# Moving work from VectorE to GpSimd and ScalarE in a two-layer diffusion trunk on one core

## The chip, the cores and the metric

The kernel runs on one core of one Trainium2 chip. A core has five engines with instruction queues of their own: TensorE (PE, matrix products; PEld is its weight load), VectorE (DVE), ScalarE (ACT), GpSimd (POOL) and SyncE (SP), which here issues every DMA. The metric is the device time of one execution in microseconds, lower is better. A time is the median of several runs; the profile comes from one further execution.

## The reference

Two layers work on 1024 latent tokens and 256 context tokens of width 1024, in float32. Cut to what matters:

```python
sh1, sc1, g1, sh2, sc2, g2 = modulation(c, w_ada[i], b_ada[i])       # silu(c) @ w_ada + b_ada, in six parts
h = modulate(rms_norm(x, norm1_g[i]), sh1, sc1)                      # the context likewise, with c_ctx
a_z, bq, bk, bv, cq, ck, cv = split_proj(h @ w_in[i])
out_a = chunk_gmlp(a_z, a_ws[i], a_bs[i])                            # gating in chunks of 128
out_b = window_attn_latent(q_b, k_b, v_b, k_bc, v_bc, b_sink[i])     # 8 heads, window 128, sink
o_c = diff_attn_latent(q_c, k_c, v_c, k_cc, v_cc, lam)               # 4 heads, two softmax maps each
x = x + g1 * (concat([out_a, out_b, out_c]) @ w_out[i])
x = x + g2 * conv_ffn(modulate(rms_norm(x, norm2_g[i]), sh2, sc2), w_up[i], conv_w[i], conv_b[i], w_down[i])
```

`conv_ffn` projects up to 2 x 2816 features, applies a depthwise convolution of width 3, multiplies silu(gate) by the value half and projects down. The context takes the same steps in layer 0 and gives keys and values only in layer 1.

## The kernel before

**Weights.** A float32 weight block comes by DMA into `raw` (three buffers). ScalarE rounds it into a high part, and a second engine subtracts the high part from the block to get the low part; both go into one tile `wsp` (three buffers, tag `ws`). `wunit` (L111) does this; its engine for the subtraction is VectorE everywhere, through the helper `sub` (L108). A product is the sum of three: high by high, high by low, low by high (`mm3`, L123), so TensorE needs a low part only at the third product of each block of 128 rows. Activations (`h`, `g`, keys, queries) are split alike.

**Modulation.** In layer 0 `mod_chunk` (L135) multiplies 2 MB chunks of `w_ada` on TensorE with a 32-column `cpad`, four 512 KB pieces a chunk, and four row blocks side by side in the array. In layer 1 `mod_wide` (L156) has VectorE multiply-add each 128 x 512 block with a column of `cpad` into an accumulator, eight blocks for each chunk and condition, then transpose and reduce it. It runs inside the MLPs of layer 0's groups b and c, called by `hook` at a given feature tile: four chunks with two conditions there, eight chunks with one here.

**Opening.** One 2 MB chunk of modulation, two context tiles (`load_x`, L322: load, square sum, transpose, store), three more chunks, the small setup, then `norms` for five tiles, `setup2` (rope tables and small constants by many small DMAs and table writes), then the input projection `ipset` with column blocks 3 and 2 of `w_in`.

**Norm.** `norm_tile` (L196) squares a tile on ScalarE, adds its eight blocks with one VectorE reduction (`red`, L203), transposes, takes a power of -0.5 on GpSimd, makes a diagonal matrix, spreads it by a product, multiplies, applies scale and shift, and splits into high and low.

**Attention.** `units_b` and `units_c` compute scores into PSUM; `negmax` (L471) copies them negated to SBUF with a running minimum on VectorE; ScalarE takes the exponential; TensorE transposes it and multiplies with the values. In `units_b` the reciprocal row sums become 128 x 128 diagonals (L569, on VectorE), used by a product (L606) after the outputs of the second half of the heads. In `units_c` the tail takes a power on GpSimd (L738).

**MLP.** `mlp` (L817) works on a group of columns (three groups in each layer, `G0` and `G1`, 256 to 516 columns wide). For each of 22 feature tiles `up` makes two products, evicts with the convolution's centre tap on ScalarE (L837) and the two side taps on VectorE (L841, L844), and forms `g`. `down` takes three or four feature tiles at a time: eight units of `w_down` of 384 or 512 columns a partition, each with 9 or 12 products and an addition into the residual `xg` (L869).

**Order.** The Tile framework places the instructions on each engine's queue with a simulated timeline, in the order of the program where several are ready; so the MLP of group a fills in beside the later tiles' attention, in both layers. Each queue then runs in that fixed order, and an instruction that waits holds what stands behind it.

## Time and profile before

| | |
|---|---|
| median of three runs | 3370.29 us (3367.59 to 3371.93) |
| profiled execution, time | 3366.29 us |
| profiled execution, span from first to last instruction | 3364.5 us |
| TensorE busy, mean granted clock | 3160.1 us (94%), 0.971 |
| VectorE busy | 2473.2 us (74%) |
| ScalarE busy | 1669.9 us (50%) |
| GpSimd busy | 368.0 us (11%) |
| DMA | 499.5 MB, 148 GB/s over the span |

A row of the groups reads: line, engine, operation, output<-inputs by the program's names with their shapes, count, then busy time in us and the mean of one in ns, then idle time of the engine just before them and what ended it. A row of the windows has the stretch, its length, the busy time of TensorE, its weight loads, VectorE, ScalarE and GpSimd with their instruction counts, the granted clock of TensorE (1.00 is full), the share of time that the DMA engines were busy, and what they moved. A row of a timeline has start, length, engine, line, operation, names and shapes, and in brackets the idle time before it with what ended it. A DMA issue is a row of the queue SPq. The profile's chain of waits covers only the later part of the span in this case, so stages are read by windows and waits.

### The profile page before, as it was taken

What the parts mean: (1) busy time and instruction counts of PE and PEld (TensorE: products, weight loads), DVE (VectorE), ACT (ScalarE), POOL (GpSimd) and SP (SyncE); (2) the same over time, 40 slices, a digit from 0 to 9 for tenths busy, and PEclk for the clock granted to TensorE, in tenths of its full rate; (3) what the DMA queues carried; (4) which work ended last, traced back from release to release, by engine and by line L of the source; (5) the groups of instructions that cost most, each with busy time, mean ns of one, the idle gap of its engine ahead of it and who ended that gap; (6) DMA issues with size and microseconds to landing.
All of it is one profiled execution on the core that took longest, in us unless ns stands there. A gap on an engine that the chain in (4) does not pass through costs nothing. (4 is left out here: it accounts for less than half of the span.)

```text
span 3364.5 us, 54283 instructions
## 1 busy us (share of the span) xinstructions
PE 3160.1 (94%) x19695; PEld 2760.8 (82%) x19695; DVE 2473.2 (74%) x5666; ACT 1669.9 (50%) x2931; POOL 368.0 (11%) x386
## 2 busy tenths in 40 slices
PE   6999988899998999999999899999999999999999
PEld 4777656787897898998999777767887789999998
DVE  4776765776888895879866578758887686676666
ACT  3555545655555443634334345557565564444443
POOL 0444200100000000100001144101000000000000
PEclk7999988899999999999999999999999999999999
DMA  9555795344442583377433555445555446334433
GB/s 270 172 157 156 222 272 149 100 117 131 126 125 78 169 250 111 103 206 210 131 93 110 161 146 159 126 142 142 155 149 148 114 124 194 112 113 135 132 115 111
DMA packets 766411, 499.50 MB, mean 148 GB/s; under 512 B 81480, under 2 KB 722368, under 8 KB 766144
## 3 DMA queue, kind: packets, MB, share of 16 engines
q1 hardware_dynamic: 766144, 496.03, 51.7%
q8 instruction: 156, 2.56, 0.3%
q14 instruction: 111, 0.91, 0.1%
HBM read 432.48 MB, written 63.44 MB: 147 GB/s over the span
## 5 line engine op out<-in xcount | busy, mean ns | idle before, releaser
L130 PE MATMUL z<-h,wsp 128*128 128x386 f32 (+3 forms) x5280 | 871.5, 318 | 12.5 <-DVE t L844 6.9
L130 PEld LDWEIGHTS z<-h,wsp 128*128 128x128 f32 x5280 | 819.4, 189 | 27.3 <-issue 9.6
L115 ACT ACTIVATE wsp<-raw 128x1024 fp32r<-128x1024 f32 (+2 forms) x660 | 555.8, 846 | 462.1 <-PE z L130 229.8
L109 DVE TENSOR_TENSOR wsp<-raw,wsp 128x1024 fp32r<-128x1024 f32 (+2 forms) x660 | 641.6, 974 | 86.6 <-ACT wsp L115 83.4
L130 PE MATMUL z<-g,wsp 128*128 128x386 f32 (+3 forms) x2640 | 459.9, 322 | 23.3 <-DVE xg L869 9.9
L130 PEld LDWEIGHTS z<-g,wsp 128*128 128x128 f32 x2640 | 416.5, 191 | 40.8 <-issue 13.2
L132 PE MATMUL z<-wsp,h 128*128 128x512 f32 x1584 | 408.3, 404 | 15.5 <-ACT wsp L115 7.3
L132 PEld LDWEIGHTS z<-wsp,h 128*128 128x128 f32 x1584 | 293.1, 192 | 84.7 <-ACT wsp L115 8.2
L130 PE MATMUL zS<-h,wsp 128*128 128x386 f32 (+1 forms) x2112 | 334.8, 314 | 8.0 <-DVE t L844 6.4
L130 PEld LDWEIGHTS zS<-h,wsp 128*128 128x128 f32 x2112 | 319.5, 191 | 10.6 <-issue 6.6
L837 ACT ACTIVATE t<-z,cw 128x386 f32<-128x386 f32 (+3 forms) x220 | 138.3, 629 | 247.2 <-PE z L130 243.8
L841 DVE SCALAR_TENSOR_TENSOR t<-z,cw,t 128x255 f32<-128x255 f32 (+3 forms) x264 | 132.7, 503 | 121.4 <-ACT t L837 120.8
L672 ACT ACTIVATE ec<-ec,nmc 128x1280 f32<-128x1280 f32 (+1 forms) x144 | 182.2, 1266 | 67.3 <-DVE ec L473 66.4
L130 PE MATMUL z<-oT,wsp 128*128 128x384 f32 (+2 forms) x1056 | 199.3, 336 | 3.1 <-DMA oT<-o_s 2.1
L473 DVE TENSOR_SCALAR_CACHE_REDUCE ec<-S,nmc 128x512 f32<-128x512 f32 (+1 forms) x256 | 156.8, 612 | 54.3 <-PE S L669 51.6
L130 PE MATMUL zS<-g,wsp 128*128 128x386 f32 (+1 forms) x1056 | 182.9, 317 | 12.0 <-DVE t L844 4.0
L130 PEld LDWEIGHTS z<-oT,wsp 128*128 128x128 f32 x1056 | 176.7, 189 | 12.0 <-DMA oT<-o_s 2.9
L669 PE MATMUL S<-Kc,qc 128*128 128x512 f32 (+1 forms) x400 | 158.7, 418 | 27.0 <-DVE ec L473 24.3
L869 DVE SCALAR_TENSOR_TENSOR xg<-z,mods,xg 128x384 f32<-128x384 f32 (+5 forms) x288 | 140.4, 501 | 58.0 <-PE z L130 57.8
L130 PEld LDWEIGHTS zS<-g,wsp 128*128 128x128 f32 x1056 | 162.7, 192 | 17.6 <-ACT wsp L115 4.6
L360 POOL TENSOR_TENSOR rs<-ss,cst 128x8 f32<-128x8 f32 (+1 forms) x76 | 116.2, 1529 | 366.6 <-DVE ss L358 293.3
L590 ACT ACTIVATE PT<-T 128x512 f32<-128x512 f32 (+1 forms) x168 | 94.7, 573 | 117.8 <-PE T L586 104.9
(245 smaller groups left out, 4450.5 us busy)
## 6 DMA issues: line engine op xcount, KB each, us to landing
raw<-in_w_up_dram SPq DMA_DIRECT2D x264, 512.0 KB
mraw<-in_w_ada_dram SPq DMA_DIRECT2D x96, 512.0 KB
raw<-in_w_down_dram SPq DMA_DIRECT2D x192, 256.0 KB
Kc<-qk_s SPq DMA_DIRECT2D x96, 320.0 KB
raw<-in_w_in_dram SPq DMA_DIRECT2D x52, 512.0 KB
raw<-in_w_out_dram SPq DMA_DIRECT2D x48, 512.0 KB
raw<-in_w_down_dram SPq DMA_DIRECT2D x104, 192.0 KB
qk_s<-st SPq DMA_DIRECT2D x18, 512.0 KB
```

The lines of the kernel that those rows point to most:

```text
L109: eng.tensor_tensor(out=lo, in0=src, in1=hi.bitcast(F32), op=ALU.subtract)
L115: act.activation(out=hl[:, 0], in_=raw, func=AF.Copy)
L130: pe.matmul(ps, w(i, k), h(j, k), start=s, stop=e)
L132: pe.matmul(ps, h(i, k), w(j, k), start=s, stop=e)
L360: pool.tensor_tensor(out=rs[:, :ns], in0=ss[:, 1, :ns], in1=mhalf[:, :ns], op=ALU.pow)
L473: dve.tensor_scalar(out=neg, in0=s_ap, scalar1=-1.0, scalar2=init, op0=ALU.mult, op1=ALU.min, accum_out=acc)
L590: act.activation(out=PT[:, :w_], in_=tp[:, :w_], func=AF.Copy)
L669: pe.matmul(S[:, :w_], q[:, m, ti * P:ti * P + P], K[m][:, o:o + w_], start=True, stop=True)
L672: act.activation(out=e[:, :nk], in_=e[:, :nk], func=AF.Exp, scale=-1.0, bias=acc, accum_out=l1[:, m, ti:ti + 1])
L837: act.activation(out=t[:, o:o + n], in_=ps[:, :n], func=AF.Identity, scale=cw[:, L, 1, ft:ft + 1], bias=cw[:, L, 3, ft:ft + 1])
L841: dve.scalar_tensor_tensor(out=t[:, o + b + 1:o + e], in0=ps[:, b:e - 1], scalar=cw[:, L, 0, ft:ft + 1], in1=t[:, o + b + 1:o + e], op0=AL ...
L869: dve.scalar_tensor_tensor(out=xs, in0=ps[:, b + o0:b + o1], scalar=mods[:, L, 40 + ct, s:s + 1], in1=xs, op0=ALU.mult, op1=ALU.add)
```

## The change

- A low part on GpSimd is made in pieces of 128 columns if it has more than 256 columns (before: more than 512). `mlp` and `prep` take the engine of the low part as an argument; three MLPs (layer 0 group a, layer 1 groups a and b) give GpSimd for `w_down`.
- The diagonals of L569 are made by GpSimd.
- In `mod_wide` the products are ScalarE's and the additions GpSimd's, through a tile with two buffers.
- In the norm the reduction over eight blocks is three additions of halves. The norm is split into a front and a back.
- In `mod_chunk` a piece is 256 rows by 512 columns instead of 512 by 256, two products of 512 columns for each piece.
- Opening: `setup` comes right after the first chunk; the fronts of the norms of tiles 8, 9 and 0 are done ahead; `w_in`'s column block 3 is asked for before the last of them, its fourth piece in a pool that now exists from the start; the convolution weights are loaded by `setup3`, after the first projections.

```diff
@@ wunit
-        if eng is pool and nk * ncol > 512:
+        if eng is pool and nk * ncol > 256:
@@ mod_chunk
-        for c in range(2):
-            for kth in range(2):
-                raw = mkraw()
-                c0 = ch * 512 + c * 256
-                sp.dma_start(out=raw, in_=a["w_ada"][L, kth * 512:kth * 512 + 512, c0:c0 + 256]
-                             .rearrange("(k p) c -> p k c", p=P))
-                for j in range(4):
-                    pe.matmul(ps[32 * j:32 * j + 32, c * 256:c * 256 + 256], cpad[:, 4 * kth + j, :], raw[:, j, :],
-                              start=(kth == 0), stop=(kth == 1))
+        for q in range(4):
+            raw = mkraw()
+            sp.dma_start(out=raw, in_=a["w_ada"][L, q * 256:q * 256 + 256, ch * 512:ch * 512 + 512]
+                         .rearrange("(k p) c -> p k c", p=P))
+            for i in range(2):
+                j = 2 * (q % 2) + i
+                pe.matmul(ps[32 * j:32 * j + 32, :], cpad[:, 2 * q + i, :], raw[:, i, :], start=(q < 2), stop=(q >= 2))
@@ mod_wide
-                        dve.tensor_scalar(out=acc[s], in0=raw[:, k], scalar1=c1, scalar2=None, op0=ALU.mult)
+                        act.activation(out=acc[s], in_=raw[:, k], func=AF.Identity, scale=c1)
                     else:
-                        dve.scalar_tensor_tensor(out=acc[s], in0=raw[:, k], scalar=c1, in1=acc[s],
-                                                        op0=ALU.mult, op1=ALU.add)
+                        pr = mktr()
+                        act.activation(out=pr, in_=raw[:, k], func=AF.Identity, scale=c1)
+                        pool.tensor_tensor(out=acc[s], in0=acc[s], in1=pr, op=ALU.add)
@@ norm_tile, now norm_front and norm_back
-            dve.tensor_reduce(out=red, in_=sq.rearrange("p k t -> p t k"), axis=AX.X, op=ALU.add)
+            for w_ in (4, 2):
+                dve.tensor_tensor(out=sq[:, 0:w_], in0=sq[:, 0:w_], in1=sq[:, w_:2 * w_], op=ALU.add)
+            dve.tensor_tensor(out=red, in0=sq[:, 0], in1=sq[:, 1], op=ALU.add)
@@ units_b, scores
-                            dve.tensor_scalar(out=dgs[ti][:, j], in0=ident, scalar1=ls[:, j:j + 1], scalar2=None,
-                                              op0=ALU.mult)
+                            pool.tensor_scalar(out=dgs[ti][:, j], in0=ident, scalar1=ls[:, j:j + 1], scalar2=None,
+                                               op0=ALU.mult)
@@ mlp, down (prep and w_out alike, with VectorE everywhere)
-                w = wunit(a["w_down"][L, fs[0] * P:fs[0] * P + nf * P, ct * P:ct * P + P], nf, P)
+                w = wunit(a["w_down"][L, fs[0] * P:fs[0] * P + nf * P, ct * P:ct * P + P], nf, P, eng=lo)
@@ norms
-        ahead = max(ahead, len(q))
+        ahead = 2 if pre else ahead
...
-            norm_tile(L, 0, xc, int(i >= NLT), h[:, 0], h[:, 1], mk, big, xc, ss, E_[eng[n % len(eng)]], add[n % len(add)])
+            if ss != "done":
+                norm_front(xc, mk, big, xc, ss)
+            norm_back(L, 0, xc, int(i >= NLT), h[:, 0], h[:, 1], E_[eng[n % len(eng)]], add[n % len(add)])
@@ opening
+    wx = mkpool("wx0", 1, "right")
...
     modset(0, (2,), ini, "mev", ini, "mraw", 16, mkz, mkU)
-    pre = [load_x(i, nwk, mkT) for i in (8, 9)]
+    setup(ini, mkU)
+
+    def load_norm(i):
+        xc, ss = load_x(i, nwk, mkT)
+        norm_front(xc, mkT, None, xc, ss)
+        return xc, "done"
+
+    pre = [load_norm(i) for i in (8, 9)]
     modset(0, (3, 0, 1), ini, "mev", ini, "mraw", 16, mkz, mkU)
-    setup(ini, mkU)
     mod_scale(0, 0)
+    w3 = inproj_w(0, 3, wx)
+    pre.append(load_norm(0))
...
     setup2(ini2, 0, mkU)
-    ipset(0, al, (3, 2))
+    ipset(0, al, (3, 2), w=w3)
+    setup3(ini2, 0, mkU)
@@ layer 0 group a, layer 1 groups a and b
-    mlp(0, G0[0], *x1, M, hook)
+    mlp(0, G0[0], *x1, M, hook, pool)
-    mlp(1, G1[0], *x1, M, hook)
+    mlp(1, G1[0], *x1, M, hook, pool)
-    mlp(1, G1[1], *st["x2"], M, hook)
+    mlp(1, G1[1], *st["x2"], M, hook, pool)
```

More of the change, by code (lines that the diff above doesn't have):

```diff
@@ L193, in mod_scale, with norm_front @@
                                      in1=g, op0=ALU.add, op1=ALU.mult)
-    def norm_tile(L, which, src, s, hi, lo, mkps, mkbig, f=None, ss=None, eng=pool, add='a'):
+    def norm_front(src, mkps, mkbig, f=None, ss=None):
         ms = sm.tile([P, 2], F32, tag="nms", name="nms")
@@ L216, in norm_tile, with norm_back @@
         dve.tensor_tensor(out=f, in0=src, in1=bc[:, 0:P].unsqueeze(1).to_broadcast([P, KT, P]), op=ALU.mult)
+        return f
+    def norm_back(L, which, f, s, hi, lo, eng=pool, add='a'):
         for k in range(KT):
@@ L224, in norm_tile @@
         sub(eng, lo, f, hi)
+    def norm_tile(L, which, src, s, hi, lo, mkps, mkbig, f=None, ss=None, eng=pool, add='a'):
+        norm_back(L, which, norm_front(src, mkps, mkbig, f, ss), s, hi, lo, eng, add)
     def setup_c(ini, ips):
@@ L309, in setup2, with setup3 @@
                                  op0=ALU.add, op1=ALU.subtract)
+    def setup3(ini, L, mkp):
         cr = ini.tile([2 * NFF, 4, P], F32, tag="cr", name="cr")
@@ L779, in prep_loads, with prep @@
         return xg, oT, [lambda k=k: load(k) for k in range(0, KT, 2)]
-    def prep(L, G, p, mp, pl=None):
+    def prep(L, G, p, mp, pl=None, lo=dve):
         wd = G["W"]
@@ L790, in prep @@
             for ct in range(KT):
-                w = wunit(a["w_out"][L][:, ct * P:ct * P + P], KT, P)
+                w = wunit(a["w_out"][L][:, ct * P:ct * P + P], KT, P, eng=lo)
                 ps = mkz()
@@ L815, in trunk, with mlp @@
     GB = 5
-    def mlp(L, G, xg, hT, halo, mp, hook=lambda f: None):
+    def mlp(L, G, xg, hT, halo, mp, hook=lambda f: None, lo=dve):
         halo()
@@ L968, in norms @@
         q = pre or [load(i) for i in tiles[:ahead]]
-        ahead = max(ahead, len(q))
+        ahead = 2 if pre else ahead
         for n, i in enumerate(tiles):
-            q += [load(j) for j in tiles[n + ahead:n + ahead + 1]]
+            q += [load(j) for j in tiles[len(q):n + ahead + 1]]
             xc, ss = q[n]
             h = hp.tile([P, 2, KT, P], F32R, tag="h", name="h")
-            norm_tile(L, 0, xc, int(i >= NLT), h[:, 0], h[:, 1], mk, big, xc, ss, E_[eng[n % len(eng)]], add[n % len(add)])
+            if ss != "done":
+                norm_front(xc, mk, big, xc, ss)
+            norm_back(L, 0, xc, int(i >= NLT), h[:, 0], h[:, 1], E_[eng[n % len(eng)]], add[n % len(add)])
             hts[i] = h
@@ L985, in modwide @@
                  lambda: p.tile([P, 512], F32, tag="mev", name="mev", bufs=2),
-                 lambda: p.tile([P, 512], F32, tag="mtr", name="mtr"))
+                 lambda: p.tile([P, 512], F32, tag="mtr", name="mtr", bufs=2))
     def modset(L, chs, evp, evt, rawp, rawt, rawb, mkps, mkpt):
@@ L990, in modset @@
             mod_chunk(L, ch, mkps, mkpt, evp.tile([P, 512], F32, tag=evt, name="mev", bufs=wb.get(evt, 1)),
-                      lambda: rawp.tile([P, 4, 256], F32, tag=rawt, name="mraw", bufs=rawb))
+                      lambda: rawp.tile([P, 2, 512], F32, tag=rawt, name="mraw", bufs=rawb))
     modset(0, (2,), ini, "mev", ini, "mraw", 16, mkz, mkU)
-    pre = [load_x(i, nwk, mkT) for i in (8, 9)]
+    setup(ini, mkU)
[4 more added lines that the diff above has]
+    pre = [load_norm(i) for i in (8, 9)]
     modset(0, (3, 0, 1), ini, "mev", ini, "mraw", 16, mkz, mkU)
-    setup(ini, mkU)
     mod_scale(0, 0)
+    w3 = inproj_w(0, 3, wx)
+    pre.append(load_norm(0))
     ini.release()
@@ L1000, in trunk @@
     wk = mkpool("wk0", 2, "right")
-    wx = mkpool("wx0", 1, "right")
     hts = {}
@@ L1034, in trunk @@
     mod_scale(0, 1)
-    wx.release()
     wk.release()
     hp.release()
+    wx.release()
     def attn(L, tiles):
@@ L1096, in hook @@
             setup2(ini, 1, mkT)
+            setup3(ini, 1, mkT)
         if f == NH[0]:
```

## The prediction

> **What bounds the kernel now.** I read the stage windows first: the span cut where the work changes, with busy time of each engine, granted clock and DMA share.
>
> ```profile
> core 0: us, PE busy (x) PEld busy (x) DVE busy (x) ACT busy (x) POOL busy (x), PEclk, DMA share, GB/s
> 0.00:60.00 60.00, 34.45 (x209) 19.01 (x210) 23.53 (x68) 17.92 (x31) 3.11 (x9) 0.74 0.92 277
> 330.00:560.00 230.00, 205.34 (x1339) 140.42 (x1339) 144.31 (x465) 115.93 (x218) 27.69 (x26) 0.93 0.78 223
> 560.00:1110.00 550.00, 521.34 (x3146) 445.36 (x3146) 425.50 (x1124) 315.16 (x560) 32.13 (x27) 0.96 0.42 116
> 1110.00:1260.00 150.00, 144.09 (x833) 137.17 (x832) 139.34 (x237) 63.37 (x100) 1.64 (x2) 1.00 0.73 222
> 1260.00:1450.00 190.00, 189.13 (x1018) 179.20 (x1016) 133.79 (x192) 87.82 (x140) 13.96 (x8) 1.00 0.37 107
> 1450.00:1660.00 210.00, 193.62 (x1513) 189.30 (x1514) 187.93 (x333) 83.26 (x131) 14.32 (x12) 0.98 0.71 203
> 1840.00:2260.00 420.00, 387.17 (x2205) 303.07 (x2204) 292.59 (x808) 202.62 (x381) 110.36 (x124) 0.95 0.52 148
> 2260.00:2760.00 500.00, 460.83 (x3378) 390.57 (x3378) 400.58 (x1035) 308.99 (x556) 28.69 (x25) 0.98 0.53 141
> 2760.00:3060.00 300.00, 291.38 (x1664) 283.77 (x1663) 206.02 (x325) 132.19 (x203) 11.51 (x8) 1.00 0.44 131
> ```
>
> TensorE is the engine that sets the end; a microsecond is won only where it stands idle or at a low clock. Its idle time is window minus busy: 25.6 us in the opening, 28.7 in layer 0's attention (560 to 1110), 5.9 and 16.4 in the two stretches with the second modulation, 39.2 in layer 1's attention (2260 to 2760), 8.6 behind it. In 1260 to 1450 VectorE is 70% busy and TensorE idles 0.9 us; in 1110 to 1260 and 1450 to 1660 VectorE is at 93% and 89%, and TensorE has holes. Second, the waits of TensorE in these stretches, one or two largest of each (total us, times, longest), in order of the stretches 560, 1450 and 2260:
>
> ```profile
> PE S L669 <- DVE ec L473: 15.7, 18, 3.8
> PE zS L130 <- DVE t L844: 10.4, 5, 3.1
> PE S L669 <- DVE ec L473: 6.5, 8, 1.6
> PE z L130 <- DVE xg L869: 5.9, 6, 2.0
> ```
>
> All name VectorE. So relief of VectorE can become time there, up to those idle sums. Third, the opening in order of time:
>
> ```profile
> 20.00:30.00 10.00, 5.56 (x56) 2.07 (x56) 1.74 (x4) 0.00 (x0) 0.00 (x0) 0.87 1.09 348
> 40.00:50.00 10.00, 5.90 (x24) 4.34 (x22) 7.42 (x24) 5.71 (x11) 1.44 (x2) 0.50 0.78 152
> 35.77 0.17 DVE L153 TENSOR_TENSOR mods<-mods,bcol 128x8 f32<-128x8 f32 x1
> 47.63 1.41 SPq L113 DMA_DIRECT2D raw<-in_w_in_dram  x3
> 52.73 0.80 PE L132 MATMUL z<-wsp,h 128*128 128x512 f32 x1 [2.58 <-ACT wsp L115]
> 52.81 4.56 SPq L293 DMA_DIRECT2D tab_ck<-tb  x2
> 67.52 1.06 ACT L115 ACTIVATE wsp<-raw 128x1024 fp32r<-128x1024 f32 x1 [6.16 <-DMA raw<-in_w_in_dram]
> 75.94 4.41 PE L132 MATMUL z<-wsp,h 128*128 128x512 f32 x18
> ```
>
> The modulation is ready at 36 us, but w_in is asked for at 47.6, behind the small loads of `setup2`; its fourth piece, behind the table writes on SP, reaches ScalarE at 67.5. TensorE projects without holes only from about 76, and meanwhile ran at 0.50.
>
> **The change part by part.** The prices, VectorE first, then GpSimd and ScalarE:
>
> ```profile
> L170 DVE SCALAR_TENSOR_TENSOR mev<-mraw,cpad,mev 128x512 f32<-128x512 f32 x112 | 83.9, 757 | 1.1 <-DMA mraw<-in_w_ada_dram 1.1
> L109 DVE TENSOR_TENSOR wsp<-raw,wsp 128x512 fp32r<-128x512 f32 x192 | 131.3, 685 | 8.5 <-ACT wsp L115 6.4
> L109 DVE TENSOR_TENSOR wsp<-raw,wsp 128x384 fp32r<-128x384 f32 x104 | 58.0, 561 | 10.0 <-ACT wsp L115 9.5
> L569 DVE TENSOR_SCALAR dgb<-cst,ls 128x128 f32<-128x128 f32 x144 | 34.5, 285 | 9.9 <-PE T L606 8.6
> L203 DVE TENSOR_REDUCE red<-nb 128x128 f32<-128x1024 f32 x28 | 55.3, 1975 | 4.3 <-ACT nb L201 4.3
> L373 DVE TENSOR_TENSOR kn<-kn,r 128x512 f32<-128x512 f32 x18 | 12.6, 698 | 0.0
> L373 DVE TENSOR_TENSOR ko<-ko,r 128x256 f32<-128x256 f32 x38 | 15.9, 420 | 0.3
> L373 DVE TENSOR_TENSOR ko<-ko,r 128x128 f32<-128x128 f32 x20 | 5.8, 288 | 0.0
> L109 POOL TENSOR_TENSOR stb<-ob,stb 128x512 fp32r<-128x512 f32 x18 | 23.8, 1324 | 431.7 <-ACT stb L612 353.0 <-DMA raw<-in_w_up_dram 32.5 <-PE S L550 27.4
> L369 POOL TENSOR_TENSOR r<-ko,tab 128x128 f32<-128x128 f32 x76 | 40.0, 548 | 49.6 <-issue 18.3 <-DVE ko L361 17.6 <-ACT sq L354 4.5
> L435 POOL TENSOR_SCALAR x<-x 128x512 f32<-128x512 f32 x18 | 15.6, 868 | 45.5 <-ACT x L434 42.4 <-DVE x L436 2.7
> L437 ACT ACTIVATE x<-x 128x512 f32<-128x512 f32 x18 | 11.3, 628 | 8.4 <-DVE x L436 8.1
> ```
>
> *Second modulation.* VectorE loses the 112 multiply-adds, 83.9 us (and 16 short first products); 128 products go to ScalarE at 0.63, 80 us, and 112 adds to GpSimd at 1.32, 148 us. Half of it (four chunks, two columns each: 8 chains of 16) lies in 1110 to 1260, half (eight chunks, one column) in 1450 to 1660: 42 us each off a VectorE with 139 and 188. GpSimd had 2 and 14 us there, and ScalarE was under half busy, so both have room. The ceiling is the idle time, 22.3 us. What is added as waits: with two buffers the third product waits on ScalarE for a GpSimd add, and behind it stand weight conversions and evictions; the transpose of a chain waits on VectorE for the last add, behind it the `t` of the MLP. A wait that is queued too early costs between 0 and one add, 1.3 us, on each of 16 chains: 0 to 21 us. I take 3, since a chain has a whole feature tile of time and the holes to fill are few: **-17 us**, with 2 more left as other waits.
>
> *Low parts of w_down* in three MLPs: 48 units each, 32 of 512 and 16 of 384 columns: 32 x 0.685 + 16 x 0.561 = 30.9 us off VectorE in each. GpSimd gets 176 pieces of 128 columns for each MLP. Such a piece isn't in the trace as a contiguous subtraction: a quarter of the 512-column one is 0.33, the strided 128-column product 0.55 us. I take 0.5, 88 us for each MLP. *Diagonals:* 34.5 us off VectorE, 144 GpSimd operations between a quarter of 0.868 (0.22) and 0.87; I take 0.4, 58 us. They are needed only by the broadcast after the second half's outputs, so transposes and value products cover them; without that cover one costs 0.4 where it cost 0.285. *Norms:* 1.975 becomes 0.698 + 0.420 + 0.288 = 1.41, 28 times: 16 us off VectorE, five or more norms in a stage.
>
> In layer 0's attention the sum is 31 + 9 (32 diagonals of two tile pairs) + 3, 43 us of 425, so VectorE goes from 77% to 70%; in layer 1's it is the same of 401, from 80% to 72%. The stage at 70% had almost no holes, which would take most of 28.7 and 39.2 us away. But the chain of scores, maximum, exponential and the 4 us for `red` stay serial. I take a third: **-9 and -13 us**. GpSimd's power operations of the norms and of the attention tail now stand behind low parts, and VectorE behind them, 0 to 2 us each time; that is a reason for a third.
>
> *Last MLP with GpSimd (2760 to 3060).* TensorE is nearly full, so there is little to win and a slower supplier can lose. The unit's pace:
>
> ```profile
> 2844.74 5.48 PE L130 MATMUL z<-g,wsp 128*128 128x386 f32 x30
> ```
>
> 12 products are 2.19 us; four pieces on GpSimd 1.3 to 2.2. At 0.5 the supply is just quicker. With some units late, and VectorE's waits there eased: **+2 us** (-4 to +10).
>
> *Opening.* w_in's third block is now asked for right behind the modulation's weights. Four chunks, two context tiles, one x tile and w_in are 8.4 + 1.0 + 0.5 + 2.1 MB = 12 MB (2.1 MB a chunk); at 348 GB/s 34.5 us, so they are in by about 40. Modulation is ready at 36 as before; shift, rounding and low part take some 4 us, and the first product starts near 40, not 52.7. With five tiles of 24 products at the pace of the quoted row (18 in 4.41), TensorE is then as far near 62 as now at 76 to 82: 14 to 20 us. What is late next: tiles 1 and 2 of x, and the rope tables, which move behind. The lead can be lost wholly to them or to later loads. **-14 us**, between 0 and -20.
>
> *Modulation of layer 0 after the opening* (eight chunks in 330 to 560). The products change from four 256-column ones side by side to two 512-column ones for each piece of the same size.
>
> ```profile
> 330.79 0.64 PE L144 MATMUL z<-mraw,cpad 128*32 128x256 f32 x8 [0.33 <-DMA mraw<-in_w_ada_dram]
> PE z L144 <- DMA mraw<-in_w_ada_dram: 9.1, 8, 2.2
> ```
>
> If two run in the time of their columns, a piece takes 1.28 and not 0.64: 32 pieces, 0 to +20 us; TensorE waits for DMA in this stage, so most hides: **+3 us**. In the opening it lies under the loads. *Layer 1's projection* (1840 to 2260): shorter norms, diagonals: **-2 us**.
>
> Sum: -14 - 17 - 9 - 13 + 2 + 3 - 2 = **-50 us**. The profiled execution took 3366.3 (span 3364.5); it becomes 3316. It lies 4.0 below the median of 3370.3, so I predict **3320**.
>
> **The rivals.** (a) *The shared port eats the relief.* GpSimd and VectorE may hinder each other. Low part on VectorE with GpSimd 52% busy (100 to 200 us), then with it at 1% (2800 to 2900):
>
> ```profile
> 100.00:200.00 100.00, 93.17 (x427) 74.83 (x425) 73.21 (x156) 52.17 (x99) 51.69 (x57) 0.97 0.53 160
> L109 DVE TENSOR_TENSOR wsp<-raw,wsp 128x1024 fp32r<-128x1024 f32 x11 | 14.4, 1327 | 1.8 <-ACT wsp L115 1.8
> L109 DVE TENSOR_TENSOR wsp<-raw,wsp 128x1024 fp32r<-128x1024 f32 x20 | 24.4, 1220 | 3.5 <-ACT wsp L115 3.5
> ```
>
> That is 9% at half load, so 4 to 5% at the quarter load that the attention stages get: about 6 us of VectorE in each, which the sum bears. If instead each such operation waits out a whole running piece, the gain of both attention stages (22 us) and 3 of the modulation go: -25, **3345**. The Trainium skill, "SBUF — State Buffer", section "Who interferes with whom", states this stronger form: a VectorE instruction with two SBUF inputs and a GpSimd instruction that reads SBUF hold an exclusive lock against each other for the whole instruction. By that rule the time is 3345; the trace's 9% shows a much milder mean.
>
> (b) *More comes through*: the attention stages fall to the holes of the 70% stage (-19, -28), the opening gives 18, the modulation 20: -85, **3285**.
>
> (c) *Slower: GpSimd becomes the bound of w_down.* A unit is fed by three or four pieces in order, behind diagonals and powers. If a piece takes 0.8 us, four are 3.2 against TensorE's 2.19; 32 such units and 16 of three pieces (2.4 against 1.64) lose 32 x 1.0 + 16 x 0.76 = 45 us in each MLP without cover; in the last of the three there is none, and half of it shows in the two beside attention: about 90 us, less the 65 that the rest wins: **3395**. It decides from 0.55 us a piece on, where four are 2.2; the strided row stands just there, the 512-column row speaks for less.
>
> (d) *No change*: relief falls where TensorE is full already, the opening's lead is lost again at the loads of 330 to 560, and the new waits of the chains cost 17: **3370**.
>
> **How the numbers follow.** Forecast 0.52, (a) 0.18, (b) 0.10, (c) 0.12, (d) 0.08. A measurement of this kernel tells about 0.2%, 6.7 us, from none. Faster: 0.52 + 0.18 + 0.10 = 0.80; same 0.08; slower 0.12. The forecast's own range is 3300 to 3342. For 8 in 10 it reaches over (a) and part of (b) and (d): **3288 to 3368**.
>
> **What would show it.** Right: first L132 product near 40 us and no holes to 70; TensorE's idle in the stretch of the second modulation under 6 us and VectorE under 70% there; L669's waits for `ec` shorter; GpSimd some 800 us busy. Wrong: TensorE waiting for GpSimd's `wsp` in the w_down units (c), `wsp` subtractions on VectorE well over 1.33 us (a), or ScalarE and VectorE waiting for GpSimd in the modulation's chains.

## The result and the profile after

| | before | after |
|---|---|---|
| median, four runs each | 3371.11 us (3367.59 to 3372.16) | 3351.89 us (3348.78 to 3354.95) |
| ratio, 95% interval | | 0.9945 [0.9928, 0.9962] |
| profiled execution, span | 3364.5 us | 3353.1 us |
| VectorE busy | 2473.2 us | 2342.6 us |
| GpSimd busy | 368.0 us | 883.6 us |

The change brings 19 us, not 50. It is faster, as forecast, and in the range, but it brings less than half of what was forecast. The profiled execution of the kernel after took 3354.95 us, the longest of its four, so the profiles are only 11 us apart. Of six runs of e1_modvec (below) one took 5291 us at a granted clock of 0.71 and is left out of its median. The same stretches as before, from the windows of the kernel after:

```profile
core 0: us, PE busy (x) PEld busy (x) DVE busy (x) ACT busy (x) POOL busy (x), PEclk, DMA share, GB/s
0.00:60.00 60.00, 39.73 (x169) 19.77 (x169) 24.32 (x65) 19.08 (x32) 2.45 (x8) 0.91 0.86 277
330.00:560.00 230.00, 214.93 (x1281) 142.11 (x1279) 147.09 (x454) 122.62 (x227) 46.85 (x56) 0.98 0.76 223
560.00:1110.00 550.00, 525.57 (x3214) 451.61 (x3214) 398.48 (x1052) 314.46 (x567) 138.12 (x235) 0.97 0.44 121
1110.00:1260.00 150.00, 133.63 (x704) 129.44 (x703) 124.06 (x152) 96.06 (x149) 89.57 (x57) 0.94 0.62 192
1450.00:1660.00 210.00, 195.47 (x1584) 191.77 (x1584) 166.90 (x250) 115.70 (x180) 98.29 (x65) 1.00 0.68 196
2260.00:2760.00 500.00, 461.99 (x3325) 390.94 (x3326) 371.47 (x962) 306.93 (x554) 134.79 (x234) 0.97 0.52 139
2760.00:3060.00 300.00, 294.59 (x1684) 287.59 (x1683) 179.12 (x273) 129.42 (x197) 92.46 (x183) 1.00 0.46 136
```

TensorE's idle time (window minus busy) goes from 25.6 to 20.3 in the opening, from 28.7 to 24.4 in layer 0's attention, from 39.2 to 38.0 in layer 1's, from 16.4 to 14.5 in the second half of the modulation. In its first half (1110 to 1260) it **grows** from 5.9 to 16.4, although 42 us of multiply-adds left VectorE there: VectorE's busy time fell only from 139.3 to 124.1. The windows are fixed in time and the kernel after is some 17 us ahead when it comes to this one, so it does somewhat later work in it. What TensorE waits for in that stretch, from the waits of the kernel after:

```profile
PE zS L130 <- DVE wsp L109: 5.0, 3, 2.9
PE T L755 <- DVE o L751: 4.0, 1, 4.0
PE zS L130 <- ACT wsp L115: 3.8, 2, 3.6
```

and VectorE's groups of the same stretch, first of the kernel after, then two of the kernel before:

```profile
L109 DVE TENSOR_TENSOR wsp<-raw,wsp 128x1024 fp32r<-128x1024 f32 x21 | 32.0, 1527 | 2.7 <-ACT wsp L115 2.7
L109 DVE TENSOR_TENSOR wsp<-raw,wsp 128x512 fp32r<-128x512 f32 x16 | 15.9, 1002 | 0.1
L862 DVE TENSOR_TENSOR t<-t,th 128x386 f32<-128x386 f32 x11 | 11.3, 1024 | 0.1
L854 DVE SCALAR_TENSOR_TENSOR t<-z,cw,t 128x385 f32<-128x385 f32 x11 | 6.8, 614 | 0.2
```

```profile
L852 DVE TENSOR_TENSOR t<-t,th 128x386 f32<-128x386 f32 x10 | 5.6, 557 | 0.0
L844 DVE SCALAR_TENSOR_TENSOR t<-z,cw,t 128x385 f32<-128x385 f32 x10 | 6.2, 616 | 0.0
```

The first three read two tensors from SBUF. The low parts of w_down have stayed on VectorE in this MLP, so they are the operations priced at 1220 and 685 ns: they now take 1527 and 1002. The product L862 (L852 before) takes 1024 ns instead of 557. The fourth reads one operand from PSUM and one from SBUF, and it is as short as before. One by one, from the timelines of VectorE and of GpSimd (start, length):

```profile
1125.62 0.62 DVE L854 SCALAR_TENSOR_TENSOR t<-z,cw,t 128x385 f32<-128x385 f32 x1
1126.16 1.81 DVE L109 TENSOR_TENSOR wsp<-raw,wsp 128x1024 fp32r<-128x1024 f32 x1
1127.89 1.62 DVE L862 TENSOR_TENSOR t<-t,th 128x386 f32<-128x386 f32 x1
1129.43 1.22 DVE L749 TENSOR_TENSOR crs<-crs,rl 128x2 f32<-128x2 f32 x1
...
1132.08 1.22 DVE L109 TENSOR_TENSOR wsp<-raw,wsp 128x1024 fp32r<-128x1024 f32 x1
...
1136.68 2.17 DVE L109 TENSOR_TENSOR wsp<-raw,wsp 128x1024 fp32r<-128x1024 f32 x1
1138.77 0.55 DVE L862 TENSOR_TENSOR t<-t,th 128x386 f32<-128x386 f32 x1
```

```profile
1125.60 8.84 POOL L170 TENSOR_TENSOR mev<-mev,mtr 128x512 f32<-128x512 f32 x5
```

Five adds run back to back on GpSimd from 1125.6 to 1134.4. Inside, a product of two columns (L749) takes 1.22 us; L862 takes 1.62 there and 0.55 at 1138.77, when no add runs. Not every operation is held up: the subtraction at 1132.08 takes 1.22 us, as without adds, and it is the mean that rises. A length that no longer follows the size suggests a wait for something shared. The price rows of the parts on GpSimd and ScalarE, whole run:

```profile
L170 POOL TENSOR_TENSOR mev<-mev,mtr 128x512 f32<-128x512 f32 x112 | 175.8, 1583 | 124.6 <-ACT mtr L169 121.7 <-DMA gt<-in_b_qnorm_dram 0.3
L109 POOL TENSOR_TENSOR wsp<-raw,wsp 128x128 fp32r<-128x128 f32 x528 | 253.9, 513 | 448.8 <-ACT wsp L115 397.2 <-DVE t L851 22.4 <-PE S L679 16.3
L579 POOL TENSOR_SCALAR dgb<-cst,ls 128x128 f32<-128x128 f32 x144 | 89.2, 632 | 372.7 <-PE T L616 182.3 <-DVE ls L577 182.1 <-issue 3.8
L169 ACT ACTIVATE mtr<-mraw,cpad 128x512 f32<-128x512 f32 x112 | 78.6, 716 | 31.1 <-POOL mev L170 25.8 <-DVE modr L174 4.2 <-DMA mraw<-in_w_ada_dram 0.7
```

An add takes 1583 ns where 1320 was priced, a piece of a low part 513 (500 priced), a diagonal 632 (400), a product on ScalarE 716 (630). ScalarE's products wait 25.8 us in all for the adds (last row).

The opening, from TensorE's and SyncE's timelines:

```profile
41.66 1.22 PE L132 MATMUL z<-wsp,h 128*128 128x512 f32 x2 [0.58 <-ACT h L228]
...
63.85 0.63 PE L345 MATMUL T<-cst,xin 128*128 128x128 f32 x4 [4.30 <-DMA xin<-in_x_dram]
...
70.58 1.22 PE L132 MATMUL z<-wsp,h 128*128 128x512 f32 x2 [2.04 <-ACT h L228]
```

```profile
51.51 2.73 SPq L301 DMA_DIRECT2D tab_ck<-tb  x2
54.29 4.08 SPq L289 DMA_DIRECT2D gt<-in_b_knorm_dram  x1
58.48 0.37 SPq L336 DMA_DIRECT2D xin<-in_x_dram  x1
```

The first product comes at 41.7 instead of 52.7. But tile 1 of x is asked for only at 58.5, behind table writes and a small load on SyncE's queue, and TensorE waits 4.3 us for it at 59.5.

### The profile page after: what moved, and what is told of

Its sections match the earlier page's. It is cut to its first block, busy times and chain, and to the rows that moved or that the text cites. A ratio compares the mean times of both kernels' runs of the same rounds, so it can differ in the third digit from the quotient of the medians.

```text
span 3353.1 us, 54588 instructions
## 1 busy us (share of the span) xinstructions
PE 3164.3 (94%) x19503; PEld 2753.6 (82%) x19503; DVE 2342.6 (70%) x5306; ACT 1744.9 (52%) x3059; POOL 883.6 (26%) x1170
## 5 line engine op out<-in xcount | busy, mean ns | idle before, releaser
L130 PE MATMUL z<-h,wsp 128*128 128x386 f32 (+3 forms) x5280 | 871.7, 318 | 20.4 <-DVE t L854 10.2
L130 PEld LDWEIGHTS z<-h,wsp 128*128 128x128 f32 x5280 | 822.0, 190 | 36.4 <-issue 13.9
L109 DVE TENSOR_TENSOR wsp<-raw,wsp 128x1024 fp32r<-128x1024 f32 (+2 forms) x516 | 565.9, 1099 | 121.3 <-ACT wsp L115 118.5
L130 PE MATMUL z<-g,wsp 128*128 128x386 f32 (+3 forms) x2640 | 463.5, 323 | 17.8 <-ACT wsp L115 5.7
L130 PEld LDWEIGHTS z<-g,wsp 128*128 128x128 f32 x2640 | 418.1, 192 | 35.8 <-issue 11.0
L132 PE MATMUL z<-wsp,h 128*128 128x512 f32 x1584 | 404.8, 402 | 13.0 <-ACT wsp L115 3.3
L109 POOL TENSOR_TENSOR wsp<-raw,wsp 128x128 fp32r<-128x128 f32 x528 | 253.9, 513 | 448.8 <-ACT wsp L115 397.2
L132 PEld LDWEIGHTS z<-wsp,h 128*128 128x128 f32 x1584 | 291.6, 191 | 79.9 <-ACT wsp L115 4.3
L130 PE MATMUL zS<-h,wsp 128*128 128x386 f32 (+1 forms) x2112 | 333.7, 313 | 8.1 <-DVE t L854 3.2
L130 PEld LDWEIGHTS zS<-h,wsp 128*128 128x128 f32 x2112 | 318.9, 190 | 10.9 <-ACT wsp L115 4.3
L170 POOL TENSOR_TENSOR mev<-mev,mtr 128x512 f32<-128x512 f32 x112 | 175.8, 1583 | 124.6 <-ACT mtr L169 121.7
L130 PE MATMUL z<-oT,wsp 128*128 128x384 f32 (+2 forms) x1056 | 200.0, 336 | 4.9 <-DMA oT<-o_s 3.4
L130 PE MATMUL zS<-g,wsp 128*128 128x386 f32 (+1 forms) x1056 | 184.4, 319 | 14.9 <-ACT wsp L115 4.3
L483 DVE TENSOR_SCALAR_CACHE_REDUCE ec<-S,nmc 128x512 f32<-128x512 f32 (+1 forms) x256 | 156.7, 612 | 56.0 <-PE S L679 52.7
L130 PEld LDWEIGHTS z<-oT,wsp 128*128 128x128 f32 x1056 | 176.1, 188 | 15.1 <-issue 4.9
L579 POOL TENSOR_SCALAR dgb<-cst,ls 128x128 f32<-128x128 f32 x144 | 89.2, 632 | 372.7 <-PE T L616 182.3
```

The costliest lines, as they stand in the source:

```text
L109: eng.tensor_tensor(out=lo, in0=src, in1=hi.bitcast(F32), op=ALU.subtract)
L130: pe.matmul(ps, w(i, k), h(j, k), start=s, stop=e)
L132: pe.matmul(ps, h(i, k), w(j, k), start=s, stop=e)
L170: pool.tensor_tensor(out=acc[s], in0=acc[s], in1=pr, op=ALU.add)
L483: dve.tensor_scalar(out=neg, in0=s_ap, scalar1=-1.0, scalar2=init, op0=ALU.mult, op1=ALU.min, accum_out=acc)
L579: pool.tensor_scalar(out=dgs[ti][:, j], in0=ident, scalar1=ls[:, j:j + 1], scalar2=None, op0=ALU.mult)
```

## Experiments

All ratios are to the kernel before on the same chip, with 95% intervals; 0.001 is 3.4 us. Several chips were used, so differences below go by the ratios. The kernel after was run again (e12_after).

| kernel | median us | ratio [interval] |
|---|---|---|
| e1_modvec: after, modulation on VectorE | 3350.53 | 0.9948 [0.9935, 0.9961] |
| e2_split: after, its first half on VectorE | 3343.07 | 0.9925 [0.9913, 0.9937] |
| e3_memset: after, two fills for each add | 3311.05 | 0.9830 [0.9817, 0.9843] |
| e8_fill3: after, three fills for each add | 3314.48 | 0.9854 [0.9836, 0.9872] |
| e4_bufs: after, five buffers | 3340.69 | 0.9922 [0.9909, 0.9935] |
| e5_lodve: after, low parts on VectorE | 3340.05 | 0.9932 [0.9916, 0.9949] |
| e6_diagdve: after, diagonals on VectorE | 3337.32 | 0.9916 [0.9900, 0.9931] |
| e9_oldchunk: after, old chunk shape | 3349.32 | 0.9945 [0.9929, 0.9961] |
| e12_after: after, again | 3347.30 | 0.9942 [0.9925, 0.9959] |
| e7_open: before, reordered opening | 3350.78 | 0.9961 [0.9948, 0.9974] |
| e13_sums: opening and norm sums | 3367.50 | 0.9997 [0.9988, 1.0006] |
| e10_nopool: opening, sums, chunk shape | 3326.34 | 0.9878 [0.9860, 0.9897] |
| e11_best: e10, second half of the modulation moved | 3328.57 | 0.9889 [0.9870, 0.9908] |
| e15_lopool: e10, low parts on GpSimd | 3324.50 | 0.9865 [0.9851, 0.9880] |
| e16_diagpool: e10, diagonals on GpSimd | 3349.19 | 0.9939 [0.9927, 0.9951] |
| e17_modpool: e10, modulation on GpSimd | 3337.96 | 0.9911 [0.9898, 0.9924] |
| e18_nudge: e10 and 24 tiny operations | 3339.76 | 0.9928 [0.9915, 0.9942] |
| e19_diagnudge: e16 and the same | 3330.73 | 0.9898 [0.9885, 0.9912] |

**The second modulation, undone.** Of L170's chain, all of it (e1_modvec) or the part with two conditions (e2_split) goes back:

```diff
-                        act.activation(out=pr, in_=raw[:, k], func=AF.Identity, scale=c1)
-                        pool.tensor_tensor(out=acc[s], in0=acc[s], in1=pr, op=ALU.add)
+                        dve.scalar_tensor_tensor(out=acc[s], in0=raw[:, k], scalar=c1, in1=acc[s],
+                                                        op0=ALU.mult, op1=ALU.add)
```

> The kernel after with the second modulation's products and sums back on VectorE (scalar_tensor_tensor, as before); all else stays. Theory (GpSimd's adds hold VectorE up: the kernel after goes into this stretch about 17 to 21 us ahead of the kernel before, loses 13 to 17 of them in its first half, 1100 to 1260, and gets some 6 back in its second, 1450 to 1660): the first half's loss goes, the second half's gain goes too, so about 3342 to 3348, and the products zS of group b stop losing to the kernel before. Rival (the move relieved VectorE as meant, and the loss has another cause, in the order of work or in an earlier stage): 3355 to 3370, slower than the kernel after.

> The kernel after with only the first half of the second modulation (two sets of columns, beside group b of layer 0) back on VectorE; its second half (one set, beside group c) stays with ScalarE and GpSimd. Theory (in the first half the adds cost 13 to 17 us, in the second they bring about 6): 3336 to 3343, the best of these four that computes everything. Rival (the loss has another cause than these adds): 3350 to 3362.

e1_modvec comes out equal to the kernel after, between the two ranges expected: as made, the moved modulation is worth nothing, where 17 us were forecast. e2_split comes out 7 us below the kernel after, at the end of the theory's range. Of my theory, the half that says TensorE's holes in the first half go away with the adds fell: they are nearly as large (150 - 135.71 = 14.3 us, from the first row of the windows of e1_modvec; 16.0 in e2_split):

```profile
1110.00:1260.00 150.00, 135.71 (x731) 131.43 (x730) 133.14 (x218) 56.82 (x86) 1.60 (x1) 0.95 0.60 187
1450.00:1660.00 210.00, 199.03 (x1606) 196.32 (x1605) 187.70 (x347) 87.99 (x138) 14.17 (x11) 0.98 0.66 189
```

**Reading or time?** The add is replaced by fills of the product's buffer, which read nothing; two are shorter than the add, three are as long.

```diff
-                        pool.tensor_tensor(out=acc[s], in0=acc[s], in1=pr, op=ALU.add)
+                        for _ in range(3):
+                            pool.memset(pr, 0.0)
```

> The kernel after with each of GpSimd's adds of the second modulation replaced by two fills of the product's buffer with zeros, which read nothing from SBUF; ScalarE still waits for GpSimd before it writes that buffer again. It leaves out the sums, so the second modulation is wrong. Theory (what is lost is that an add that reads SBUF keeps VectorE's operations with two SBUF inputs from starting): w_down's subtraction of 128x1024 goes back from about 1.8 to 2.2 us to 1.2 to 1.3 us beside GpSimd, and the time to 3325 to 3338, since the relief of 42 us of VectorE's work in each half now reaches TensorE. Rival (ScalarE's in-order wait for GpSimd's buffers, or GpSimd's load on any port): 3346 to 3356 with the subtraction as long as in the kernel after.

> As the kernel with two fills in place of each add of the second modulation, but with three fills, about 1.58 us, so that GpSimd is as long at each step as with the add (1583 ns in the kernel after) and ScalarE has to wait as long for the buffer; nothing of it reads SBUF. It leaves out the sums. Theory (VectorE loses by what GpSimd reads, not by GpSimd's time): 3308 to 3322. Rival (the 40 us between the fill kernel, 3311, and the kernel after came from GpSimd's being free sooner, and with it ScalarE's): 3335 to 3352.

Windows of e8_fill3, then its groups in the first stretch:

```profile
1110.00:1260.00 150.00, 146.60 (x822) 144.17 (x821) 111.68 (x177) 103.41 (x162) 84.65 (x169) 1.00 0.67 204
1450.00:1660.00 210.00, 202.63 (x1658) 200.90 (x1657) 149.03 (x274) 120.90 (x191) 95.65 (x178) 0.98 0.62 178
```

```profile
L109 DVE TENSOR_TENSOR wsp<-raw,wsp 128x1024 fp32r<-128x1024 f32 x22 | 26.8, 1217 | 3.5 <-ACT wsp L115 3.4
L109 DVE TENSOR_TENSOR wsp<-raw,wsp 128x512 fp32r<-128x512 f32 x22 | 15.0, 686 | 3.5 <-ACT wsp L115 3.2
L171 POOL MEMSET mtr<- 128x512 f32 x168 | 84.0, 527 | 38.6 <-ACT mtr L169 34.5
```

GpSimd is nearly as busy as with the adds (84.65 against 89.57 us in the first stretch, 95.65 against 98.29 in the second), yet the subtractions are back at 1217 and 686 ns, TensorE's holes fall to 3.4 and 7.4 us, and the time is 30 us (three fills) or 38 us (two) below the kernel after. So the subtractions are longer by what GpSimd reads, and not by its time.

The same work can be compared from the first product of group b's MLP in layer 0 (L130, tile `zS`) to the first of layer 1's projection (L132, tile `zS`); the whole second modulation lies between them. In order: the kernel before, e1_modvec, the kernel after, e8_fill3.

```profile
1113.40:1815.80 702.40, 679.24 (x4636) 658.48 (x4636) 564.82 (x935) 297.29 (x465) 29.92 (x22) 0.99 0.53 156
1090.20:1795.80 705.60, 678.15 (x4604) 657.57 (x4605) 555.06 (x940) 295.89 (x458) 28.90 (x21) 0.99 0.53 157
1096.50:1805.60 709.10, 677.48 (x4604) 657.25 (x4605) 538.22 (x812) 375.36 (x586) 202.12 (x133) 0.99 0.53 156
1096.10:1779.90 683.80, 670.88 (x4605) 653.48 (x4606) 483.51 (x812) 375.45 (x586) 193.97 (x357) 1.00 0.55 162
```

With the same 812 operations left to VectorE, they take 483.5 us beside fills and 538.2 beside adds. So of the 72 us by which e8_fill3 is below e1_modvec, 55 come back as longer operations. The stretch itself takes 703 to 712 us in all seven profiles with both halves on GpSimd, and 702 to 712 in eight of nine with all of it on VectorE (the ninth, e19_diagnudge: 694.5); with fills it takes 678 and 684.

A limit of the test: with fills, the serial chain of adds is gone too, and ScalarE waits less for GpSimd (15.7 against 25.8 us in this stretch). VectorE's transposes wait only 0.8 us for the last adds in the kernel after, so the chain's end is not what costs; ScalarE's wait is tried next.

**ScalarE's wait.**

```diff
-                 lambda: p.tile([P, 512], F32, tag="mtr", name="mtr", bufs=2))
+                 lambda: p.tile([P, 512], F32, tag="mtr", name="mtr", bufs=5))
```

> The kernel after with five buffers instead of two between ScalarE's products and GpSimd's adds of the second modulation. Theory (the adds' reading holds VectorE up, however long ScalarE waits): 3347 to 3357, as the kernel after. Rival (ScalarE stands in its queue before a full buffer and what is behind it comes late): ScalarE's waits for GpSimd there shrink and the time falls to 3335 to 3343.

ScalarE's idle time before its products in 1090 to 1260 that GpSimd ended falls from 11.7 to 3.8 us, and the time by 8 us, as the rival said; but TensorE's holes there do not fall (150 - 132.85 = 17.2), and the stretch from group b to layer 1 is 6 us shorter, 703.0, where fills take off 25 and more:

```profile
1110.00:1260.00 150.00, 132.85 (x704) 128.66 (x703) 120.46 (x155) 91.75 (x144) 87.26 (x56) 0.95 0.61 187
```

**The attention parts, undone** (`, pool)` taken off three calls of `mlp`; `pool.tensor_scalar` of L579 back to `dve`).

> The kernel after with w_down's low parts back on VectorE in the three MLPs that had given them to GpSimd. Forecast of record (the relief of the two attention stages is worth 9 and 13 us, the last MLP costs 2): 3365 to 3374, slower than the kernel after (3352). Theory now (VectorE's work fell there, but what remains is stretched by GpSimd's reads and TensorE's end of the stage did not move): 3346 to 3358, no difference to the kernel after.

> The kernel after with the scaled diagonals of attention back on VectorE. Theory now (they hold VectorE up as much as they relieve it, 632 ns each on GpSimd): 3347 to 3357. If they were worth a part of the 22 us of the forecast: 3358 to 3366. Rival (on GpSimd they are late in the chain of a heads' pair, and cost): 3338 to 3345.

Undone, the two parts make the kernel faster by 4 and 10 us, with intervals that touch that of the kernel after; neither shows any of the 22 us of relief. e5_lodve lies below every range expected, e6_diagdve just under its rival's.

**The opening alone** (the diff without the changes of `mod_chunk`, `mod_wide`, `red`, L579 and `lo`).

> The kernel before with the reordered opening alone (earlier first weights, front halves of the norms, the small loads of the setup moved), and nothing given to GpSimd or ScalarE, with the old shape of the modulation chunks. Forecast of record: 14 us less than before, 3352 to 3357 where before is 3369. Theory now (the first product comes 11 us earlier, but the weights' fourth piece and the tiles 1 and 2 of x are late, so that the lead at the 120th product is gone): 3358 to 3367.

13 us in the total, near the forecast of record (14) and not my later theory; whether by its mechanism is asked below.

**The rest.** If 13 of 19 us are the opening, and the parts on GpSimd bring nothing, the chunk shape and the norm's sums come next, and a kernel with all but the parts on GpSimd.

> The kernel after with the old pieces of layer 0's modulation chunks (sixteen products of 32x256 from pieces of 256 columns instead of eight of 32x512). Forecast of record (the new shape costs 3): 3343 to 3350. Theory now (the opening alone brings 13 us and the kernel after 19, although the parts on GpSimd bring nothing or cost, so the rest, chunk shape and norm sums, must bring some 6 to 19): 3355 to 3367.

> The kernel before with the reordered opening, the new chunk shape and the norm's sums by halves, and nothing at all given to GpSimd or ScalarE: modulation, diagonals and low parts all on VectorE. Theory now (what went to GpSimd brings nothing in sum; the diagonals cost up to 10, the low parts about 4, the modulation 0): 3330 to 3343, some 10 to 20 below the kernel after. Rival (the opening is all there is, or GpSimd's share does help): 3348 to 3358.

> The kernel of the run before (nothing on GpSimd) with only the second half of the second modulation, beside group c of layer 0, on ScalarE and GpSimd, with five buffers between them. Theory (there VectorE has no room, and the relief is larger than what GpSimd's reads take): 6 to 12 us below the kernel without any GpSimd share, the fastest of all that compute everything. Rival (the gain of the second half came only from what the first half had delayed): the same as that kernel within 4 us.

> The kernel after again, unchanged, so that the three others are compared with it on one chip: 0.993 to 0.996 of the kernel before, 3345 to 3358.

The kernel without any GpSimd share is 21 us faster than the kernel after, more than expected. The second half of the modulation moved alone brings nothing on top, as the rival said: TensorE starts layer 1's projection 10 us earlier than in e10_nopool (1787.9 against 1797.7) and group b's MLP there 3 us later (2684.4 against 2681.5). The old chunk shape costs the kernel after nothing.

> The kernel before with the reordered opening and the norm's sums by halves, but the old shape of the modulation chunks. Theory (the 28 us between the opening alone and the kernel with no GpSimd share come from the norm's sums, since the chunk's old shape cost the kernel after nothing): ratio 0.987 to 0.990, some 3324 to 3335. Rival (they come from the chunk shape): 0.994 to 0.997, 3348 to 3358. If both have a part, or the order of work that follows from them, it lies between.

> The kernel with no GpSimd share, with the low parts of w_down on GpSimd in the three MLPs, as in the kernel after. Forecast of record (20 us of relief): 3304 to 3310. Theory now (GpSimd's reads take as much from VectorE's operations with two SBUF inputs as they relieve, and the pieces come later): 3328 to 3342, 2 to 15 slower than without.

> The kernel with no GpSimd share, with attention's scaled diagonals on GpSimd, as in the kernel after. Forecast of record (part of 22 us of relief): below 3322. Theory now (a diagonal takes longer there and the products wait for it): 3329 to 3340, 3 to 13 slower than without. Rival (no effect): within 3 us of it.

> The kernel with no GpSimd share, with the second modulation on ScalarE and GpSimd with two buffers, as in the kernel after. Forecast of record: 17 us below it, 3306 to 3312. Theory now (loss in its first half, gain in its second): within 6 us of it, 3320 to 3334, with 10 to 20 us lost beside group b and 6 to 10 won beside group c.

e13_sums and e16_diagpool are slower than any range expected. e17_modpool misses too: it is 11 us slower than e10_nopool, but starts layer 1's projection 5 us before it (1792.7 against 1797.7). It falls behind only later, to 12.5 us at group b's MLP in layer 1 (2694.0 against 2681.5), in stages that the edit leaves alone. e15_lopool misses both expectations: the low parts on GpSimd neither cost nor bring (-4 us, inside the intervals). In its windows and those of e10_nopool (second fence), VectorE is 19 and 17 us less busy in the two attention stretches, and TensorE's idle time falls by 0.8 and 3.7 us:

```profile
560.00:1110.00 550.00, 529.64 (x3246) 455.59 (x3246) 407.70 (x1093) 317.88 (x575) 118.46 (x203) 0.97 0.45 122
2260.00:2760.00 500.00, 473.95 (x3446) 405.10 (x3443) 386.50 (x993) 314.13 (x568) 130.83 (x232) 0.99 0.51 141
```

```profile
560.00:1110.00 550.00, 528.88 (x3236) 456.50 (x3237) 426.90 (x1131) 315.68 (x570) 31.41 (x27) 0.97 0.44 121
2260.00:2760.00 500.00, 470.30 (x3397) 402.25 (x3396) 403.58 (x1030) 310.10 (x560) 30.48 (x26) 0.98 0.51 138
```

The differences do not add up: the diagonals cost 10 us undone and 21 added; the chunk shape 0 undone, while the new shape brings 40 from e13_sums to e10_nopool; the norm's sums, which take work off VectorE, cost 12 (e7_open to e13_sums). The last pair asks whether the planner's order is a term by itself. 24 operations of two columns are added, 0.22 us each and 5.4 us in all (some 1.5 were expected). Compared by the names of the tiles, the order of TensorE's 19503 products then differs in 1862 lines between e10_nopool and e18_nudge, and in 3770 between e16_diagpool and e19_diagnudge:

```diff
                         dve.reciprocal(out=l2, in_=l2)
+                        st["nud"] = st.get("nud", 0) + 1
+                        if st["nud"] % 3 == 0:
+                            dve.tensor_scalar(out=l2, in0=l2, scalar1=1.0, scalar2=None, op0=ALU.mult)
```

> The kernel with no GpSimd share, with one more tiny operation of VectorE (two columns times 1.0) behind every third reciprocal of attention, 24 in all, some 1.5 us of VectorE's time. It computes the same; the planner orders hundreds of instructions otherwise. Theory A (a part of the differences between the experiments is the order that the planner happens to choose): 8 us or more away from the kernel without it, 3326. Theory B (the order is of no weight, the parts differ by their own cost): 3323 to 3331.

> The same tiny operations in the kernel that has the diagonals on GpSimd and nothing else there. Theory A (order): 8 us or more away from 3349, perhaps back near 3330. Theory B (the diagonals themselves cost 21 us on GpSimd): 3346 to 3353, and 18 to 26 above the other kernel of this pair.

One becomes 17 us slower, the other 14 us faster, and their rank turns round. Layer 1's attention and first MLP in e10_nopool, then in e18_nudge:

```profile
2280.00:2700.00 420.00, 394.00 (x2929) 338.09 (x2926) 345.14 (x885) 264.56 (x475) 23.93 (x20) 0.98 0.54 148
```

```profile
2280.00:2700.00 420.00, 387.78 (x2889) 330.48 (x2887) 345.46 (x898) 263.60 (x478) 24.97 (x21) 0.98 0.54 147
```

VectorE's work is the same (345.1 and 345.5 us) and TensorE does 40 products fewer in the same time. The added work is the same in both pairs, and the times move in opposite directions, so its own cost can't be the reason. **The order that the planner happens to choose is worth about 15 us either way in these two pairs**. Differences of up to some 20 us above, between kernels whose order differs, are not shown to be the cost of the part that was edited; that holds for e7_open's 13 us and the 21 us between e10_nopool and the kernel after as for e2_split, e4_bufs, e5_lodve, e6_diagdve, e11_best, e13_sums, e16_diagpool and e17_modpool. The 40 us between e13_sums and e10_nopool are larger than either shift; 28 of the 44 us between their profiles arise behind group a's first MLP product (613.6 and 597.1 us), where the edited chunks no longer run, so that order may have much of these too. Repeating one kernel is much tighter (0.9945 and 0.9942 for the kernel after, in two separate measurements).

## Why the prediction was right or wrong

**Opening, -14: right in size, but not by its mechanism.** Alone it brings 13. The first product comes at 41.7 in the kernel after (forecast: near 40; the modulation is ready at 38.8, not 36) and at 45.6 in e7_open, and the step named what is late next: tiles 1 and 2 of x. "No holes to 70" failed: there is one of 4.3 us. The step wanted TensorE 14 to 20 us ahead after 120 products. It misread the kernel before, whose 120th product of L132 starts at 92.6 us and not at 76 to 82, and at the quoted pace 120 products from 40 end near 69, not 62. In e7_open the lead of 7.1 us at the first product is 1.2 at the 120th and 0.4 at the 240th (122.2 us). It is 8.5 at group a's first MLP product (607.2 against 615.7) and 12.7 at group b's, when little of the edited opening is left to run. e13_sums has the same opening, with the norm's sums, and ends level with the kernel before. So the agreement is, as far as the runs show, largely luck.

**Second modulation, -17: the step that failed.** It measured 0: e1_modvec equals the kernel after, and the stretch that holds it takes as long with it on GpSimd as on VectorE, in kernels of many different orders. The relief was real as long as nothing was read: with fills, in kernels that leave out the sums, TensorE's idle time is 3.4 us in the first half (the forecast asked for under 6) and 7.4 in the second. What was mis-sized is the price: I charged the move with its waits, "a wait that is queued too early", 3 us, and not with what 112 adds that read SBUF do to VectorE's own operations, 55 us of its time in that stretch. VectorE stayed at 83% and 79% in the two halves where under 70% was the sign of being right, and ScalarE did wait for GpSimd (25.8 us), a sign of being wrong; with five buffers that wait is mostly gone and the holes of the first half stay. The growth of the first half's holes from 5.9 to 16.4 us is not the adds' doing: they are 14.3 and 12.3 in e1_modvec and e10_nopool, without any add on GpSimd. Rival (a) had the mechanism, but was priced with its main loss in the attention stages and "3 of the modulation", from a row in which GpSimd is 52% busy and the mean subtraction loses 9%. In 1110 to 1260 GpSimd is 60% busy with instructions of 1.6 us back to back, and the mean subtraction loses 25% (1527 against 1220), the small ones more. The mean over a stage of shorter GpSimd operations was the wrong row for one of long ones. The Trainium skill, "SBUF — State Buffer", section "Who interferes with whom", has it as it came: a VectorE operation with two SBUF inputs contends with a GpSimd operation that reads SBUF, one with a single SBUF input and outside the two-port modes doesn't, and GpSimd's pure writes don't count. This trace agrees where it can be read: 1527 against 1220 ns, 614 against 616 with one operand from PSUM, 1217 ns beside fills. One operation with a single SBUF input did wait (L745, last section); whether it ran in a two-port mode no run shows.

**Attention, -9 and -13: did not come.** A piece at 513 ns was right, a diagonal at 632 not (400 taken, 870 the upper end), nor a norm's sum, 1.68 us instead of 1.41 (745, 457 and 481 ns). VectorE's busy time fell by 27 and 29 us of the 43, and the idle time of TensorE by 4.2 and 1.2 us. "A third" of the idle time was the failing step: e15_lopool takes 19 and 17 us off VectorE and TensorE's idle time stays within 4 us. L669's waits for `ec` (L679 in the kernel after) did get shorter, 15.7 to 11.3 us in layer 0, without moving the end; from e10_nopool to e15_lopool they go from 8.6 to 9.1 in layer 0 and from 6.9 to 6.4 in layer 1. That fits waits at the end of a serial chain, of which the step itself warned, rather than a queue that is too long; no run separates the two further.

**Last MLP, +2; layer 0's chunks, +3; layer 1's projection, -2.** In the stretch of the last MLP the idle time falls from 8.6 to 5.4, where +2 us were forecast, and no wait of TensorE for GpSimd's `wsp` is among its largest. For the second e9_oldchunk equals the kernel after, and the idle time falls from 24.7 to 15.1 in 330 to 560. The third is below what can be told. None of the three can be told from the order.

**The rivals.** The result, 3352, is nearest to (a), 3345, by the mechanism that (a) names, in a place where it was taken to be cheap; with an order worth 15 us the closeness of the number is partly luck. (b) falls. (c) falls as priced: a piece takes 0.513 us, and it was to decide from 0.55 on, although GpSimd's low parts hold 0.8% of the span in the chain that ended last. Its sum was wrong too: the terms other than the last MLP win 52 us and not 65, which gives 3408. (d) falls as a number, but the opening's lead was lost again, as it said, and earlier.

**The sum.** Modulation 0; opening and attention shares nothing that can be told from the order. How the 19 us divide stays open, as does the split of the 28 us between e7_open and e10_nopool. A term was missing altogether: the order, about 15 us of either sign, as large as the terms of -9, -13, -14 and -17 themselves. The range of 80 us was wide enough to hold it.

**Beyond the change.** e10_nopool (0.9878) and e15_lopool (0.9865) beat both kernels. Their lead over the kernel after is in part the luck of an order: with 5.4 us of work added, e10_nopool is at 0.9928. From group a's first MLP product in layer 1 to group b's, these two take 394.7 and 395.3 us, e8_fill3 397.8 and all other kernels 403 to 414.

## What to carry to other kernels

Before work goes from VectorE to GpSimd, list VectorE's operations with two SBUF inputs in that stretch and GpSimd's reads beside them; count each overlap as a wait and not as free relief, the more the longer the GpSimd instruction. Here 55 of 72 us came back that way. Relief of an engine counts only where its queue is late: a wait that names the engine need not shrink when the engine gets less to do, as in the attention of both layers here. Compare stages by the same work, from one product to another, as well as by the clock. Where a planner orders the instructions, nudge it with work worth next to nothing and see how far the time moves, before any single edit of that size is believed. A total that agrees is no proof of the step: follow the lead from product to product, as for the opening.

## What the runs showed of the hardware

A VectorE product of two columns took 0.15 us alone and up to 1.26 us beside GpSimd's adds: the wait does not go with the size of VectorE's instruction. The operation behind it, which multiplies two columns by a constant and reads one tensor, took 1.23 us, where the same operation took 0.17 before; so one SBUF input does not always spare an operation.

```profile
1120.87 0.15 DVE L744 TENSOR_TENSOR css<-css,rl 128x2 f32<-128x2 f32 x1
1122.07 1.26 DVE L744 TENSOR_TENSOR css<-css,rl 128x2 f32<-128x2 f32 x1
1123.36 1.23 DVE L745 TENSOR_SCALAR css<-css 128x2 f32<-128x2 f32 x1
```

The wait can be as long as GpSimd's instruction. In e8_fill3 a product that takes 0.56 us elsewhere took 2.57 beside one subtraction of 128x1024 on GpSimd:

```profile
1386.22 2.53 POOL L109 TENSOR_TENSOR h<-nb,h 128x1024 fp32r<-128x1024 f32 x1 [11.54 <-ACT h L229]
1386.60 2.57 DVE L863 TENSOR_TENSOR t<-t,th 128x386 f32<-128x386 f32 x1
```

Three fills of 128x512 on GpSimd, 527 ns each, leave VectorE's subtractions at 1217 and 686 ns, as long as without them.
